# Three of the four late gate blocks issued ahead of the sparse attention, each in a PSUM bank of its own

## The chip, the cores and the metric

One core of one Trainium2 chip runs the kernel. The metric is the device time of one execution in microseconds (us). The core's engines are named here as the profile names them: PE (TensorE, matmuls), PEld (its weight loads), DVE (VectorE), ACT (ScalarE), POOL (GpSimd) and SP (SyncE, whose queue issues nearly all transfers; SPq in the rows). Sums of matmuls are formed in PSUM, eight banks of 128x512 float32.

## The reference

A decoder block on 1024 tokens of width 1024, float32. Cut to what matters here:

```python
hn = rms_norm(h, attn_norm_g[l])
proj = hn @ w_in[l]
aq, ak, av, bq, bkv, iq, ik, iw, gates = jnp.split(proj, IN_SPLITS, axis=-1)
gates = jax.nn.sigmoid((gates + b_gates[l]).astype(jnp.float32)).astype(h.dtype)
gate_a, gate_b = jnp.split(gates, 2, axis=-1)
o_a = sliding_window_sink_attention(aq, ak, av, sinks[l], bias_a)
...
o_b = indexed_sparse_mla(q_abs, c_kv, iq, ik, iw, w_uv[l], bias_b)
mixed = gate_a * (o_a @ w_branch_a[l]) + gate_b * (o_b @ w_branch_b[l])
h = h + mixed @ w_out[l]
h = h + (jax.nn.silu(hn @ w_ffn_gate[l]) * (hn @ w_ffn_up[l])) @ w_ffn_down[l]
```

The gates are 2048 columns of the projection: 16 blocks of 128 columns, each for two halves of 512 tokens. Nothing but `mixed` reads them.

## The kernel before

Float32 products are made of three matmuls on split operands (high, low): high by high, high by low, low by high. A gate block for one half of the tokens is 8 slices of the width by 3, so 24 matmuls of 128x512 into one PSUM bank (`gate`, L905; `mm3`, L202, L193). Then ACT takes the tanh out of the bank (L914), POOL scales it (L915) and SP stores it in DRAM (L916, `gate_dram`). Its weights come in two chunks (`weights`, L168): SP loads a raw chunk of 256 KB (L185, `w_raw`, two buffers), ACT makes the high part (L187, `w_hi`), POOL the low part (L188, `w_lo`); the split parts have four buffers, so two blocks' weights are there at a time.

The program runs in phases. `phase1` has the projections, the choice of keys and the window attention; in it `gates` (L894) makes 28 of the 32 gate blocks as filler between other matmuls. Blocks 12 to 15 of the second half (`LATE = 4`) are left for `phase_b` (L919), the sparse attention. That phase has four pairs of heads, four units of 256 queries in each (`sparse_block`, L983). For each pair `keys_values` (L951) loads keys and values: the two heads' keys one after the other through one raw buffer `kraw` (ACT casts `kb`, L689, DVE takes the low part, L690), the values through `vraw` (L960 to L962), the meta tokens' values through `mraw` (L967 to L970). `queries` (L973) loads `qraw` and splits it on ACT (L979) and DVE (L980). A unit then has scores on PE (L1007, banks `s`), the masked row minimum on DVE (L1011, `pb`), the exponential on ACT (L1014), transposes on PE (L1038, banks `tp`) with the split on ACT and DVE (L127, L133), and the weighted values on PE (L1049 to L1052, bank `pv`). In this phase the banks are three `s`, three `tp`, one `pv` and one `gps` (the gates and branch A).

The order is found by a scheduler at build time from the order in which the program is written, the readiness of operands and buffers, and marks: a matmul issued with a mark may not be placed before the instruction that the mark names. Each engine then runs its own list in that order. `branch_a` (L1074), written behind the 16 units, makes the four late blocks and then branch A's product; its matmuls are filler for the units. Of the 96 gate matmuls the first 30 (`LFREE`) have no mark, the other 66 have marks spread over the first fifth (`LEND`) of the marked matmuls of the phase:

```python
n = LATE * KC * 3
marks = iter([self.marks[int(len(self.marks) * LEND * (i - LFREE) / (n - LFREE))] if i >= LFREE else None for i in range(n)])
for c in range(16 - LATE, 16):
    self.gate(c, 1, self.gate_weights(c), marks)
```

Branch A's own matmuls have marks from 0.1 to 0.85 of the phase, behind the loads of the window attention's output (`wa_raw`, L1065), which go into the buffers of the normed input that the last gate block frees.

Of the kernel before, what the change touches and what calls it, by code (L numbers as in the profile page):

```python
# [21 lines left out]
KC = D // P  # L22
# [34 lines left out]
GSP = (64, 180, 250)  # L57
GEND = 0.97
LATE = 4
LFREE = 30  # L60
LEND = 0.2
B2 = (0.85, 1.1)

# [40 lines left out]
class Program:  # L104
# [797 lines left out]
            for half in range(2 if c < 16 - LATE else 1):  # L902
                self.gate(c, half, w, marks, 2 * c + half >= MMG)

    def gate(self, c, half, w, marks, both=False):  # L905

        nc = self.nc
        b0 = self.col["b_gates"]
        self.turn = not self.turn
        pool, tag = (self.mm, "ps") if both and self.turn else (self.gp, "gps")  # L910
        ps = pool.tile([P, 512], F32, name=tag, tag=tag)
        self.feature_cols(ps, w, slice(0, P), NM + 512 * half, 512, marks)
        t = self.wg.tile([P, 512], F32, name="gt", tag="gt", bufs=2)
        nc.scalar.activation(t, ps, AF.Tanh, scale=0.5, bias=self.vec[:, b0 + c:b0 + c + 1])  # L914
        nc.gpsimd.tensor_scalar(t, t, 0.5, 0.5, op0=ALU.mult, op1=ALU.add)  # L915
        nc.sync.dma_start(self.gate_dram[half][c], t)  # L916


    def phase_b(self):  # L919
        nc, I = self.nc, self.I  # L920
        self.psum(0, *BP, 1, 1)
        self.marks = []
        with self.pool("kv", side="right") as kvp, self.pool("slb", side="right") as wp:
            qlo = [wp.tile([P, 2, 256], F32R, name=f"qlo{k}") for k in range(2)]
            for t in qlo:
                self.clear_lo(t)
            first = self.queries(wp, 0, ORDER[0][0], qlo[0])
            pm = [wp.tile([P, 256], F32R, name=f"pm{k}") for k in range(4)]
            self.vm = [wp.tile([P, 2, P], F32R, name=f"vm{k}") for k in range(2)]
            for t in self.vm:  # L930
                self.clear(t.rearrange("p h d -> p (h d)"))
            for t in pm:
                self.clear(t)
            self.unit, self.mixed, self.wb = 0, [], {}
            kv = self.keys_values(kvp, 0)
            for pr in range(4):
                kb, vb = kv
                bt = wp.tile([P, 2, 256], F32, name="bt_b", tag="bt_b", bufs=2)
                self.load_bias(bt, 1, 2 * pr)
                for i, sb in enumerate(ORDER[pr]):  # L940
                    q = self.queries(wp, pr, sb, qlo[i % 2]) if pr + i else first
                    self.sparse_block(wp, pr, sb, q, kb, vb, pm, bt)
                    if i == 0 and pr < 3:
                        kv = self.keys_values(kvp, pr + 1)
            self.branch_a()
            n = KC * 4 * 3
            at = [B2[0] + (B2[1] - B2[0]) * i / n for i in range(n)]
            self.branch_b(0, self.wg, iter([self.marks[min(len(self.marks) - 1, int(len(self.marks) * a))] for a in at]))
        self.mask_es.close()
# [124 lines left out]
    def branch_a(self):  # L1074

        nc, I = self.nc, self.I
        n = LATE * KC * 3
        marks = iter([self.marks[int(len(self.marks) * LEND * (i - LFREE) / (n - LFREE))] if i >= LFREE else None for i in range(n)])
        for c in range(16 - LATE, 16):
            self.gate(c, 1, self.gate_weights(c), marks)  # L1080
        pool = self.wg
        o = [self.load_o(pool, [self.oa_dram[half][:, c] for c in range(4)], 2, lo_pool=False, ring=self.xhp) for half in range(2)]
        n = KC * 2 * 4 * 3
        b0 = BSP[0]
        marks = iter([self.marks[int(len(self.marks) * (b0 + (BSP[1] - b0) * i / n))] for i in range(n)])
        for m in range(KC):
            w = self.weights(pool, I["w_branch_a"][0][:, P * m:P * m + P].rearrange("(k p) n -> p k n", p=P), raw_pool=pool, unit=512, bufs=WB)
            for half in range(2):
                hc = slice(512 * half, 512 * half + 512)
                ps = self.gp.tile([P, 512], F32, name="gps", tag="gps")  # L1090
                self.mm3(ps, [(*w[k], *o[half][k]) for k in range(4)],
                         marks)
                t = pool.tile([P, 512], F32, name="gt", tag="gt", bufs=2)
                g = pool.tile([P, 512], F32, name="ga", tag="ga", bufs=2)
                nc.sync.dma_start(g, self.gate_dram[half][m])
                nc.scalar.copy(t, ps)
                nc.gpsimd.tensor_mul(t, t, g)
                nc.sync.dma_start(self.ya_dram[half][m], t)
# [450 lines left out]
```

## Time and profile before

| | |
|---|---|
| median of 3 runs | 1499.91 us (1499.42 to 1502.9) |
| the profiled execution | 1500.29 us, span 1498.5 us |
| PE busy | 1388.4 us, 93% of the span |
| DVE / ACT / POOL busy | 990.8 / 818.1 / 648.8 us (66 / 55 / 43%) |
| granted TensorE clock, mean | 0.969 of full |
| first and last scores of the sparse attention (L1007) | 498.1 and 683.5 us |

The span is what the trace covers, from its first instruction to its last. The profiled execution took 1.8 us more than its span and lies 0.4 us above the median of the runs.

### The profile page before, as it was taken

Reading aid. Unit: us, or ns where it says so; the run is one execution under the profiler, and the core shown is the slowest. Engines: PE = TensorE matmul, PEld = TensorE weight load, DVE = VectorE, ACT = ScalarE, POOL = GpSimd, SP = SyncE. Lnnn points to the kernel's source line nnn. Section 1 sums busy time; section 2 is a strip of 40 time slices with the busy share of each in tenths; the row PEclk is TensorE's granted clock in tenths of the full one; section 3 lists DMA queues with packets and bytes.
Section 4 is the critical chain, followed back from the end, with each engine's and each line's share of the span. In section 5 each row is a group of like instructions: output and inputs, shape, how many; then the busy total and the mean of one; then the engine's idle time right before and its main releaser. Section 6 shows DMA issues by size and latency. Waiting matters only on the chain.

```text
span 1498.5 us, 21232 instructions
## 1 busy us (share of the span) xinstructions
PE 1388.4 (93%) x6847; PEld 1157.7 (77%) x6847; DVE 990.8 (66%) x2122; ACT 818.1 (55%) x1743; POOL 648.8 (43%) x823
## 2 busy tenths in 40 slices
PE   4999787999799799999899699999999999999997
PEld 3988785777587688888687478888888888888886
DVE  6258998036576787777697995444544447696585
ACT  5347684994688677886335643333333333444473
POOL 4137465666666557675300015555555555000004
PEclk9999888999899899999999899999999999999999
DMA  6421121246443845335931133332333338832332
GB/s 202 142 68 39 29 65 43 87 135 209 112 140 105 212 133 173 119 117 179 308 138 57 56 112 102 103 109 95 105 106 106 106 102 292 323 99 98 117 109 113
DMA packets 148038, 189.79 MB, mean 127 GB/s; under 512 B 11331, under 2 KB 95126, under 8 KB 147670
## 3 DMA queue, kind: packets, MB, share of 16 engines
q1 hardware_dynamic: 147568, 188.28, 39.1%
q8 instruction: 54, 0.88, 0.3%
q14 instruction: 58, 0.48, 0.1%
q10 hardware_dynamic: 198, 0.14, 0.0%
q0 software_dynamic: 160, 0.01, 0.0%
HBM read 133.49 MB, written 58.03 MB: 128 GB/s over the span
## 4 chain that ended last, share of the span: by engine, by line
PE 64%; DVE 14%; issue 6%; ACT 6%; DMA 5%; POOL 5%; SPq 1%; POOLq 0%; ACTq 0%; DVEq 0%
PE ps L193 25%; PE s L193 23%; PE gps L193 7%; DVE mask L815 4%; ACT mask L857 2%; PE pv L1049 2%; PE s L1007 2%; PE tp L1038 2%; DMA ga<-gate_dram 1%; PE tp L198 1%; POOL y L1510 1%; PE pv L193 1%; DMA kraw<-bk_dram 1%; DMA wa_raw<-in_w_in 1%; DVE hb L1267 1%
## 5 line engine op out<-in xcount | busy, mean ns | idle before, releaser
L1360 POOL TENSOR_TENSOR fhl<-fr,fhl 128x512 fp32r<-128x512 f32 x60 | 97.5, 1645 | 223.0 <-ACT fhl L1359 223.0
L1360 POOL TENSOR_TENSOR fhl<-fs,fhl 128x512 fp32r<-128x512 f32 x80 | 106.5, 1355 | 106.8 <-ACT fhl L1359 106.8
L188 POOL TENSOR_TENSOR w_lo<-w_raw,w_hi 128x512 fp32r<-128x512 f32 x60 | 81.2, 1356 | 93.9 <-ACT w_hi L187 75.8
L193 PE MATMUL s<-ht,fhl 128*128 128x512 f32 x384 | 121.8, 393 | 0.0
L193 PE MATMUL ps<-ht,fhl 128*128 128x512 f32 x320 | 101.1, 392 | 0.0
L193 PE MATMUL gps<-oh,w_hi 128*128 128x512 f32 x232 | 94.2, 406 | 4.1 <-ACT gt L914 4.1
L857 ACT ACTIVATE mask<-high,smallg 128x784 bf16<-128x784 uint16 (+3 forms) x66 | 70.2, 1063 | 46.1 <-POOL smallg L866 28.4
L193 PE MATMUL gps<-ol,w_hi 128*128 128x512 f32 x232 | 92.7, 399 | 0.0
L193 PE MATMUL gps<-oh,w_lo 128*128 128x512 f32 x232 | 92.1, 397 | 0.0
L193 PE MATMUL s<-yhl,fhl 128*128 128x512 f32 x396 | 90.6, 389 | 0.0
L193 PE MATMUL ps<-yhl,fhl 128*128 128x512 f32 x396 | 90.2, 389 | 0.0
L1430 ACT CAST yhl<-wd 128x512 fp32r<-128x512 f32 x66 | 41.1, 622 | 89.9 <-PE ps L193 50.2
L193 PE MATMUL s<-h,fhl 128*128 128x512 f32 x272 | 87.7, 393 | 0.8 <-DVE hb L1267 0.5
L193 PE MATMUL ps<-h,fhl 128*128 128x512 f32 x256 | 82.9, 395 | 5.1 <-ACT h L1317 5.1
L133 DVE TENSOR_TENSOR ptl<-tp,pth 128x512 fp32r<-128x512 f32 (+2 forms) x112 | 70.9, 645 | 23.9 <-ACT pth L127 22.6
L193 PEld LDWEIGHTS s<-yhl,fhl 128*128 128x128 f32 x396 | 74.3, 188 | 15.5
L193 PEld LDWEIGHTS ps<-yhl,fhl 128*128 128x128 f32 x396 | 74.3, 188 | 15.4
L193 PEld LDWEIGHTS s<-ht,fhl 128*128 128x128 f32 x384 | 72.0, 188 | 17.2 <-ACT fhl L1359 0.7
L865 POOL TENSOR_SCALAR smallg<-smallg 128x1 f32<-128x1 f32 x128 | 58.9, 463 | 59.9 <-ACT mask L857 59.5
L1359 ACT CAST fhl<-fr 128x512 fp32r<-128x512 f32 x66 | 39.8, 619 | 76.6 <-issue 36.1
L1431 DVE TENSOR_TENSOR yhl<-wd,yhl 128x512 fp32r<-128x512 f32 x66 | 45.6, 691 | 50.2 <-ACT yhl L1430 50.2
L193 PE MATMUL s<-lt,fhl 128*128 128x512 f32 x192 | 75.3, 392 | 0.0
(479 smaller groups left out, 4267.5 us busy)
## 6 DMA issues: line engine op xcount, KB each, us to landing
fr<-in_w_ffn_gate SPq DMA_DIRECT2D x22, 512.0 KB, 4.0
fr<-in_w_ffn_up SPq DMA_DIRECT2D x22, 512.0 KB, 4.5
wd<-in_w_ffn_down SPq DMA_DIRECT2D x44, 256.0 KB, 5.1
da<-acts SPq DMA_DIRECT2D x44, 256.0 KB, 3.6
w_raw<-in_w_in SPq DMA_DIRECT2D x40, 256.0 KB, 3.0
act<-a SPq DMA_DIRECT2D x33, 256.0 KB, 2.1
da<-act SPq DMA_DIRECT2D x33, 256.0 KB, 4.3
acts<-s SPq DMA_DIRECT2D x33, 256.0 KB, 2.0
```

The lines of the kernel that those rows point to most:

```text
L133: nc.vector.tensor_sub(lo, ps, hi.bitcast(F32))
L188: (nc.vector if lo_dve else nc.gpsimd).tensor_sub(t[1], t[2], t[0].bitcast(F32))
L193: mm = self.nc.tensor.matmul(*args, **kw)
L815: nc.vector.tensor_scalar(self.mask[j], src[j], at[:, i:i + 1], None, op0=op, op1=ALU.add, accum_out=out[:, i:i + 1])
L857: nc.scalar.activation(self.mask[j], src[j], AF.Sign, bias=at[:, i:i + 1], scale=scale, accum_out=out[:, i:i + 1])
L865: g.tensor_scalar(c[:, o], acc[:, o], bar[:, o], b[:, o], op0=ALU.is_ge, op1=ALU.subtract)
L1007: nc.tensor.matmul(ps[:, :n], q[k][:, h, qc:qc + P], kb[:, h, at:at + n], start=k == 0, stop=k == 1)
L1038: mm = nc.tensor.transpose(pt[:, P * i:P * i + P], prs[par, e][:, NM + P * rr:NM + P * rr + P], self.ident)
L1359: nc.scalar.copy(hi, a[name])
L1360: (nc.gpsimd if q else nc.vector).tensor_sub(lo, a[name], hi.bitcast(F32))
L1430: nc.scalar.copy(hi, src)
L1431: nc.vector.tensor_sub(lo, src, hi.bitcast(F32))
```

## The change

The constant `LFREE` goes. Before the sparse attention's first `keys_values`, blocks 12, 13 and 14 are written with no mark, in the banks `gps`, `tp` and `s`. Block 15 stays in `branch_a`, its 24 matmuls with marks over the same first fifth.

```diff
-LFREE = 30
...
-    def gate(self, c, half, w, marks, both=False):
+    def gate(self, c, half, w, marks, both=False, bank=None):
...
-        pool, tag = (self.mm, "ps") if both and self.turn else (self.gp, "gps")
+        pool, tag = bank or ((self.mm, "ps") if both and self.turn else (self.gp, "gps"))
...
             self.unit, self.mixed, self.wb = 0, [], {}
+            for c, ring in zip(range(16 - LATE, 16), ((self.gp, "gps"), (self.tp, "tp"), (self.sp, "s"))):
+                self.gate(c, 1, self.gate_weights(c), iter([None] * 3 * KC), bank=ring)
             kv = self.keys_values(kvp, 0)
...
-        n = LATE * KC * 3
-        marks = iter([self.marks[int(len(self.marks) * LEND * (i - LFREE) / (n - LFREE))] if i >= LFREE else None for i in range(n)])
-        for c in range(16 - LATE, 16):
+        n = (LATE - 3) * KC * 3
+        marks = iter([self.marks[int(len(self.marks) * LEND * i / n)] for i in range(n)])
+        for c in range(19 - LATE, 16):
             self.gate(c, 1, self.gate_weights(c), marks)
```

The number of instructions on each engine stays the same. The lists of the engines are alike up to the last block of the window attention and differ from there through the first four units. Counted from the first late gate matmul, the filler matmuls (gates and branch A) in PE's list stand like this at the end of units 1 to 5: before 35, 48, 72, 108, 144, with the change 74, 82, 91, 108, 144; behind the fourth unit the counts stay within 2 of each other. Line numbers of the change lie 1 lower up to L931 and 1 higher from there to L1075.

First place, PE at the end of the window attention. `pv_4078` is its last product; `gps_7662` before is block 12, and in the change `gps_5160` is block 12 and `tp_5201` block 13. Before:

```order
L193 MATMUL gps_5071<-xt0_198,w_lo_5066 128x512
L193 MATMUL pv_4078<-pth_4084,va_3070 128x512
L193 MATMUL pv_4078<-ptl_4085,va_3070 128x512
L193 MATMUL pv_4078<-pth_4095,va_3070 128x512
L193 MATMUL pv_4078<-ptl_4096,va_3070 128x512
L193 MATMUL gps_7662<-oh_182,w_hi_7650 128x512
L193 MATMUL gps_7662<-ol_183,w_hi_7650 128x512
```

and with the change:

```order
L192 MATMUL tp_5201<-oh_188,w_lo_5190 128x512
L192 MATMUL pv_4078<-pth_4084,va_3070 128x512
L192 MATMUL pv_4078<-ptl_4085,va_3070 128x512
L192 MATMUL pv_4078<-pth_4095,va_3070 128x512
L192 MATMUL pv_4078<-ptl_4096,va_3070 128x512
L192 MATMUL tp_5201<-oh_190,w_hi_5195 128x512
L192 MATMUL tp_5201<-ol_191,w_hi_5195 128x512
L192 MATMUL gps_5160<-oh_182,w_hi_5148 128x512
```

Twelve matmuls of block 13 now stand ahead of the window attention's last product and two behind it; block 12 follows them with its 24, then the other 10 of block 13 and the 24 of block 14, and only then the first scores.

Second place, ACT from the tanh of the last block of `phase1` (`gt_5096`) to the first queries (`qhi_5133`). `w_hi_7732` before and `w_hi_5230` in the change are the first chunk of block 14's weights; its buffer is the one that block 12's first chunk leaves. Before:

```order
L914 ACTIVATE gt_5096<-gps_5071,vec_281 128x512
L759 COPY o_4101<-pv_4078 64x256 x2
L689 CAST kb_5148<-kraw_5150 128x1040
L187 CAST w_hi_7732<-w_raw_7734 128x512
L961 CAST vb_5149<-vraw_5160 128x16x64
L187 CAST w_hi_7738<-w_raw_7740 128x512
L914 ACTIVATE gt_7687<-gps_7662,vec_281 128x512
L969 CAST vm0_5140<-mraw_5164 16x64 x2
L979 CAST qhi_5133<-qraw_5130 128x512
L689 CAST kb_5148<-kraw_5155 128x1040
```

and with the change, with `w_hi_7773` and `w_hi_7779` for block 15:

```order
L186 CAST w_hi_5230<-w_raw_5232 128x512
L688 CAST kb_5271<-kraw_5273 128x1040
L758 COPY o_4101<-pv_4078 64x256
L962 CAST vb_5272<-vraw_5283 128x16x64
L758 COPY o_4101<-pv_4078 64x256
L186 CAST w_hi_5236<-w_raw_5238 128x512
L688 CAST kb_5271<-kraw_5278 128x1040
L186 CAST w_hi_7773<-w_raw_7775 128x512
L913 ACTIVATE gt_5185<-gps_5160,vec_281 128x512
L962 CAST vb_5390<-vraw_5401 128x16x64
L186 CAST w_hi_7779<-w_raw_7781 128x512
L913 ACTIVATE gt_5226<-tp_5201,vec_281 128x512
```

The cast for block 14 moved ahead of the first keys' cast, and five more casts and tanhs of the gates, with the next pair's values (`vb_5390`), stand ahead of the first queries, which follow two rows further on. On DVE the first row minimum before stands behind the second head's keys (`kb_5148`); in the change the zero fills stand behind those keys, and the next pair's keys (`kb_5389`) ahead of the first row minimum.

Third place, SP's queue from the first head's keys (`kraw_5150` before, `kraw_5273` in the change) to the first queries and the next pair's keys (`kraw_5391` in the change). Before:

```order
L916 DMA gate_dram015_124<-gt_5096 128x512
L967 DMA mraw_5164<-bv_dram_82 16x64
L751 DMA oa_dram1_84<-o_4101 128x2x128
L185 DMA w_raw_7740<-in_w_in 128x4x128
L660 DMA kraw_5155<-bk_dram0_78 64x1040
L660 DMA qraw_5130<-bq_dram00_68 64x2x256 x2
L660 DMA kraw_5155<-bk_dram0_78 64x1040
L300 DMA bt_b_5171<-bias_dram1_487 128x2x256
```

and with the change:

```order
L184 DMA w_raw_7775<-in_w_in 128x4x128
L659 DMA kraw_5278<-bk_dram0_78 64x1040 x2
L961 DMA vraw_5401<-bv_dram_82 128x8x128
L750 DMA oa_dram1_84<-o_4101 128x2x128
L184 DMA w_raw_7781<-in_w_in 128x4x128
L659 DMA qraw_5130<-bq_dram00_68 64x2x256 x2
L299 DMA bt_b_5294<-bias_dram1_487 128x2x256
L659 DMA kraw_5391<-bk_dram1_79 64x1040
L915 DMA gate_dram112_137<-gt_5185 128x512
L659 DMA kraw_5391<-bk_dram1_79 64x1040
```

Both chunks of block 15 (`w_raw_7775`, `w_raw_7781`) and the next pair's values now stand ahead of the first queries, and the store of block 12 stands between the two halves of the next pair's keys.

## Rows read from the trace of the kernel before

**Rows 1.** The page: the span, and each engine's busy us, share and instructions.
```profile
span 1498.5 us, 21232 instructions
...
PE 1388.4 (93%) x6847; PEld 1157.7 (77%) x6847; DVE 990.8 (66%) x2122; ACT 818.1 (55%) x1743; POOL 648.8 (43%) x823
```

**Rows 2.** Windows: stretch, length, busy us of each engine (instructions), PEclk, DMA share, GB/s.
```profile
498.50:509.80 11.30, 7.55 (x30) 5.75 (x29) 10.02 (x28) 8.62 (x22) 9.18 (x16) 0.68 0.96 235
...
518.70:562.00 43.30, 40.86 (x253) 36.40 (x254) 36.57 (x110) 33.24 (x65) 22.34 (x37) 0.96 0.46 131
...
540.00:552.00 12.00, 12.00 (x77) 10.74 (x76) 11.54 (x30) 10.46 (x19) 6.03 (x9) 1.00 0.64 183
```

**Rows 3.** Timeline of PE: start us, us, instruction, [idle before <-releaser].
```profile
485.41 0.47 PE L193 MATMUL pv<-pth,va 128*128 128x512 f32 x1 [0.24 <-DVE o L760]
...
486.42 0.49 PE L193 MATMUL gps<-oh,w_hi 128*128 128x512 f32 x1
...
491.75 0.39 PE L193 MATMUL gps<-oh,w_lo 128*128 128x512 f32 x1
495.81 0.79 PE L193 MATMUL gps<-oh,w_hi 128*128 128x512 f32 x1 [3.68 <-ACT gt L914]
...
498.54 0.59 PE L1007 MATMUL s<-kb,qhi 128*128 128x144 f32 x2
```

**Rows 4.** Timeline of ACT at the start of the sparse attention.
```profile
489.33 1.07 ACT L689 CAST kb<-kraw 128x1040 fp32r<-128x1040 f32 x1 [1.49 <-DMA kraw<-bk_dram]
...
492.22 1.04 ACT L961 CAST vb<-vraw 128x1024 fp32r<-128x1024 f32 x1 [1.31 <-DMA vraw<-bv_dram]
494.43 0.62 ACT L187 CAST w_hi<-w_raw 128x512 fp32r<-128x512 f32 x1 [1.16 <-DMA w_raw<-in_w_in]
495.07 0.69 ACT L914 ACTIVATE gt<-gps,vec 128x512 f32<-128x512 f32 x1
...
497.18 0.62 ACT L979 CAST qhi<-qraw 128x512 fp32r<-128x512 f32 x1
...
502.07 0.41 ACT L1014 ACTIVATE pb<-pb,st 128x144 f32<-128x144 f32 x1
...
515.39 1.06 ACT L689 CAST kb<-kraw 128x1040 fp32r<-128x1040 f32 x1 [1.70 <-DMA kraw<-bk_dram]
```

**Rows 5.** Timeline of DVE, the same stretch.
```profile
490.43 1.24 DVE L690 TENSOR_TENSOR kb<-kraw,kb 64x1040 fp32r<-64x1040 f32 x1 [2.14 <-ACT kb L689]
...
494.56 0.76 DVE L155 CAST qlo<-zero 64x512 fp32r<-64x512 f32 x2
...
498.20 0.68 DVE L980 TENSOR_TENSOR qlo<-qraw,qhi 64x512 fp32r<-64x512 f32 x1
...
500.95 0.31 DVE L1011 CUSTOM_DVE_ANT_0 pb<-s,near 128x144 f32<-128x144 f32 x1
...
516.49 1.24 DVE L690 TENSOR_TENSOR kb<-kraw,kb 64x1040 fp32r<-64x1040 f32 x1 [1.28 <-ACT kb L689]
...
518.69 0.47 DVE L1011 CUSTOM_DVE_ANT_0 pb<-s,mask,st 128x256 f32<-128x256 f32 x1
```

**Rows 6.** Timeline of POOL: a gate's low weights, and the scaling of a gate.
```profile
495.12 1.33 POOL L188 TENSOR_TENSOR w_lo<-w_raw,w_hi 128x512 fp32r<-128x512 f32 x1 [2.04 <-ACT w_hi L187]
496.42 0.66 POOL L915 TENSOR_SCALAR gt<-gt 128x512 f32<-128x512 f32 x1
```

**Rows 7.** Timeline of SP's queue: when the key and query loads were issued.
```profile
491.70 0.45 SPq L660 DMA_DIRECT2D kraw<-bk_dram  x1
492.20 1.26 SPq L660 DMA_DIRECT2D qraw<-bq_dram  x2
493.50 0.60 SPq L660 DMA_DIRECT2D kraw<-bk_dram  x1
```

**Rows 8.** DMA issues from 470 to 530 us: KB each, median us to landing.
```profile
kraw<-bk_dram SPq DMA_DIRECT2D x10, 260.0 KB, 3.6
qraw<-bq_dram SPq DMA_DIRECT2D x14, 128.0 KB, 3.9
...
vraw<-bv_dram SPq DMA_DIRECT2D x3, 512.0 KB, 5.9
```

## The prediction

> **What bounds the kernel now.** I read the page first: PE is busy 93% of the span [rows 1], so a change that leaves PE's work as it is can only move PE's idle time and its clock. The windows say where that idle time lies. From 518.7 to 562 us, four units long, PE is busy 40.86 of 43.30 us [rows 2]; there the filler matmuls cost their full time. At the start of the sparse attention it is otherwise: from 498.5 to 509.8 us PE is busy 7.55 of 11.30 us at a granted clock of 0.68, so for part of the time at its lower level of 1.2 GHz, with the transfers busy at 0.96 and DVE for 10.02 us [rows 2]. In PE's timeline the reader sees the idle time just before it: gate block 12 runs from 486.42 to 491.75, then PE stands for 3.68 us until the tanh has emptied the one bank [rows 3]. ACT's timeline tells why: the tanh stood at 495.07 behind a weight cast at 494.43, which had waited 1.16 us for its load [rows 4], though the bank had been full since about 492.
>
> In block 12 twenty-three steps take 491.75 - 486.42 = 5.33 us [rows 3], so a gate matmul at full clock is **0.232 us**. PE was free for late gates at 485.41 - 0.24 = 485.17.
>
> **The change, part by part.** All instructions stay; what changes is where the 72 matmuls of three blocks, their casts, tanhs, scalings, stores and weight loads stand. There are two terms: a later start of the sparse attention, and less filler in its third and fourth unit.
>
> *Term A, the start.* PE itself would be through with its three blocks at 485.17 + 76 x 0.232 = 502.8 (72 of them and four products of the window attention). But ACT's list now holds block 14's first cast ahead of the first keys' cast. Its buffer is free only when block 12's first 12 matmuls are done, and PE has 12 of block 13, 4 products and 2 more of block 13 ahead of these: 485.17 + 30 x 0.232 = 492.1, where before that buffer was left at 486.42 + 12 x 0.232 = 489.2 and nothing waited. ACT's keys then end at 492.1 + 0.62 + 1.07 = 493.8 (0.62 and 1.07 from [rows 4]); before, at 490.4. From there one raw key buffer sets the pace:
>
> - DVE's low part, 1.24 [rows 5]: 495.1. SP issues the second head's keys twice, 0.45 each [rows 7]: 496.0. They land 3.6 later [rows 8]: 499.6. ACT casts them, 1.06 [rows 4]: 500.7.
> - Behind that cast, ACT has block 15's first chunk, 0.62, and block 12's tanh, 0.69 [rows 4]: 502.0. POOL makes the low weights, 1.33, then the scaled gate, 0.66 [rows 6], with the memsets between: about 503.6.
> - SP's list has the gate's store between the two halves of the next pair's keys. Store and second half take about 0.9: 504.5. Landing, 3.6: 508.1. ACT's cast 1.06 and DVE's low part 1.24: **510.4**. This low part stands ahead of the first row minimum on DVE, which before began at 500.95 [rows 5].
>
> So the first row minimum comes 510.4 - 500.95 = **9.5 us later**, by the list alone. Beside this chain, and hidden by it, run the first queries: block 14's second cast and block 15's load are through by about 498, the loads of the queries take 1.26 and 3.9 [rows 7, 8], landing near 503.5; the next pair's values, issued before them, land near 502.8 (5.9 [rows 8]) and ACT has values 1.04, cast 0.62, tanh 0.69 and queries 0.62 [rows 4] ahead, so the queries are split near 507. DVE's zero fills, 3.6 us from 494.56 to 498.20 [rows 5], moved behind the second keys, and end near 505. If the key chain were shorter, these would set the start at about 508. The banks cost nothing: block 14's tanh empties its scores bank right behind the last key cast, before 510.4.
>
> The keys that are early now are not waited for later: the idle 1.70 us of ACT and 1.28 us of DVE at 515.39 and 516.49 [rows 4, 5], on the way to the third unit's row minimum at 518.69, go. What is late next there is DVE's own work of two units, so I take 1.5 back: **+8** at 518.7, with 9.5 and 6.5 (both idle pieces gone) as ends.
>
> *Term B, the filler.* By the two lists, 40 late filler matmuls stood ahead of that row minimum, and 77 now; at the end of the fourth unit both have 108. So 37 x 0.232 = 8.6 us of filler leave the stretch 518.7 to 562. They free their full time only until another engine bounds the stretch. DVE has 36.57 us of work in its 43.30 [rows 2], so at most 6.7 can go; at the least nothing, if PE's idle time only grows. In the twelve microseconds of this phase where DVE is best filled it reaches 11.54 of 12.00, 96% [rows 2]. I take 94%, near that end because DVE's order is not disturbed here: 36.57 / 0.94 = 38.9, a gain of **4.4**.
>
> Behind the fourth unit the lists agree within two matmuls, so the shift stays. Sum: 8 - 4.4 = +3.6, on the profiled 1500.29 that is **1503.9 us**. The profiled execution lies 0.4 us above the median of the runs.
>
> One rule bears on term A. The row shows that a ready tanh stood behind a cast that waited for its load [rows 4]. The Trainium skill (PSUM — Partial Sum Buffer, section Engine vs sequencer instructions) says that the queues of ScalarE, VectorE and GpSimdE are strictly first in, first out; the trace agrees, by that 1.16 us. Could ACT pass a waiting instruction, the sum would be that of the first rival.
>
> **The rivals.**
>
> *Faster.* The waits that I add up along the lists may be shorter: the landing of 3.6 us was measured while the transfers were busy at 0.96 [rows 2], and the loads now stand further apart. If the start is set by PE alone, it is 502.8 - 500.95, about +2, and term B at its bound gives -6.7: -4.7, **1495.6 us**. For it: PE has no 3.68 us of idle time any more, and works without a stop to 502.8. Then the clock may hold too: 7.55 busy us at 0.68 would be 7.55 x 0.68 = 5.1 at full, 2.4 us less, for 1493.2. Against it: the single raw key buffer. It decides whether the first exponential, at 502.07 before [rows 4], comes before about 504. The Trainium skill (TensorE: Matmul & The Clock Gate, section HAM oscillation — how this bites in real kernels) has idle stretches drop the array to half rate; the window at 0.68 agrees, and by that rule the unbroken gates speak for this rival up to 502.8, my own gap behind them against it.
>
> *Slower.* The start is late by 9.5 and nothing comes back: PE has no filler in the gap between its gates' end at 502.8 and the first scores, and little in units 1 to 4, the clock falls as it did at 0.68 [rows 2], and the chain from keys over DVE and ACT to the transposes sets units 3 and 4 in place of PE. Then 1500.3 + 9.5 = **1509.8 us**. It decides if PE's busy share in those units falls while they take their 43 us as before. For it: PE's 0.96 clock there already shows some loss. Against it: DVE's 84% in that stretch leaves room.
>
> *Nothing.* The late start is just what the missing filler gives back, since the filler had only filled PE's waiting time anyway: **1500.3 us**. It is so where PE's total idle time up to the end of unit 4 stays alike; then the first row minimum is late by 4 to 7 us and unit 4 ends at 562.
>
> **How the numbers follow.** About 0.3%, 4.5 us, is what a measurement of this kernel can tell from no change; same thus reaches from 1495.4 to 1504.4. My forecast has a chance of 0.45; its own range, 1500.1 (+6.5 - 6.7) to 1507.6 (+9.5 less half of 4.4), lies 0.27 within and 0.18 above. The faster rival has 0.22, of which 0.18 is beyond the bound; the slower 0.18, 0.17 beyond; the hidden one 0.15, with 0.02 faster. Faster 0.20, same 0.45, slower 0.35. The range goes from 1494.4, the middle of the first rival's two values, to 1509.8, the second's.
>
> **What would show each step.** Right, if ACT in the changed trace idles before block 14's cast until near 492 and names PE; if the second head's keys are cast near 500; if PE has a gap from about 503 and the first row minimum comes near 510; if units 3 and 4 then take about 39 us with DVE above 90% and no idle time of ACT and DVE for keys. Term A is wrong if the first exponential comes before 506, term B if PE is still above 94% busy in units 3 and 4. The whole is wrong if the stretch behind the fourth unit, whose lists agree, changes by more than a microsecond or two.

## The result, and the profile after

The changed kernel is slower: 1509.26 us median of 6 runs (1506.78 to 1510.69) against 1501.4 us of 6 runs of the kernel before, ratio 1.0055 (95% interval 1.0042 to 1.0069). Two more sets of the same pair, below, gave 1.0022 (1.0003 to 1.0040) and 1.0030 (1.0017 to 1.0043). By all three it costs some 3 to 8 us (the lowest interval begins at 0.5); 3.6 were forecast.

The page of the changed kernel, span and engines, answers to [rows 1]:

```profile
span 1507.4 us, 21231 instructions
PE 1394.8 (93%) x6847; PEld 1161.8 (77%) x6847; DVE 997.3 (66%) x2122; ACT 818.3 (54%) x1743; POOL 648.2 (43%) x823
```

The shares tell nothing. The traces do, once both have the same zero. I count from the tanh of the last block of `phase1` on ACT, at 485.66 us before and here at:

```profile
488.20 0.69 ACT L913 ACTIVATE gt<-gps,vec 128x512 f32<-128x512 f32 x1
```

What lies ahead of that instruction is alike in both programs; its place is scatter, as the repeats show. A unit's end is taken where its last product with the meta tokens' values begins. From the tanh, in us, with the repeats' traces as second and third value:

| | before | change | later by (means) |
|---|---|---|---|
| first row minimum (DVE) | 15.3, 14.8 | 23.4, 22.7, 23.3 | 8.1 |
| row minimum that opens the third unit's rows | 33.0, 32.7 | 39.3, 39.0, 39.5 | 6.4 |
| unit 4 ends (PE) | 80.8, 80.6 | 86.5, 86.2, 88.4 | 6.3 |
| unit 5 ends | 102.8, 103.5 | 105.1, 104.8, 107.0 | 2.5 |
| unit 8 ends | 133.3, 135.0 | 135.4, 135.0, 137.2 | 1.7 |
| unit 16 ends | 219.9, 221.6 | 223.9, 223.6, 225.8 | 3.7 |
| first store of the next stage (`h_dram`, SP) | 319.0, 321.2 | 322.0, 324.6, 325.2 | 3.8 |

At the ends of these units equally many filler matmuls are done in both (108 at the fourth, 144 at the fifth, 324 at the sixteenth), so the last column compares like with like there.

**The start.** ACT's timeline of the changed kernel answers to [rows 4]:

```profile
490.31 0.62 ACT L186 CAST w_hi<-w_raw 128x512 fp32r<-128x512 f32 x1 [1.42 <-POOL gt L914]
...
492.39 1.06 ACT L688 CAST kb<-kraw 128x1040 fp32r<-128x1040 f32 x1 [1.47 <-DMA kraw<-bk_dram]
...
499.67 1.06 ACT L688 CAST kb<-kraw 128x1040 fp32r<-128x1040 f32 x1 [2.88 <-DMA kraw<-bk_dram]
...
506.34 0.62 ACT L980 CAST qhi<-qraw 128x512 fp32r<-128x512 f32 x1
508.13 1.06 ACT L688 CAST kb<-kraw 128x1040 fp32r<-128x1040 f32 x1 [1.18 <-DMA kraw<-bk_dram]
...
511.95 0.41 ACT L1015 ACTIVATE pb<-pb,st 128x144 f32<-128x144 f32 x1 [0.68 <-DVE st L1012]
```

The cast for block 14 did not hold the first keys: it ran at 490.31, right behind PE's twelfth matmul of block 13 (490.06), and the keys' cast then waited 1.47 us for its own load. The row names POOL as releaser, whose scaling ended at 490.13. Block 12's first matmul began only at 491.67, so the buffer that this cast filled can't be the one that block 12's first chunk leaves, as the change was described; by the times it is block 13's. DVE's timeline, which answers to [rows 5], shows what set the start:

```profile
493.49 1.24 DVE L689 TENSOR_TENSOR kb<-kraw,kb 64x1040 fp32r<-64x1040 f32 x1 [5.68 <-ACT kb L688]
...
500.77 1.24 DVE L689 TENSOR_TENSOR kb<-kraw,kb 64x1040 fp32r<-64x1040 f32 x1 [3.31 <-ACT kb L688]
501.93 2.56 DVE L154 CAST qlo<-zero 64x512 fp32r<-64x512 f32 x2
504.50 1.89 DVE L150 CAST vm<-zero 128x256 fp32r<-128x256 f32 x2
506.31 1.13 DVE L150 CAST pm<-zero 128x256 fp32r<-128x256 f32 x4
507.36 1.47 DVE L963 TENSOR_TENSOR vb<-vraw,vb 128x1024 fp32r<-128x1024 f32 x1
508.75 1.15 DVE L981 TENSOR_TENSOR qlo<-qraw,qhi 64x512 fp32r<-64x512 f32 x1
509.94 1.63 DVE L689 TENSOR_TENSOR kb<-kraw,kb 64x1040 fp32r<-64x1040 f32 x1
511.60 0.31 DVE L1012 CUSTOM_DVE_ANT_0 pb<-s,near 128x144 f32<-128x144 f32 x1
```

DVE stands 5.68 and 3.31 us for keys, and from 500.77 works without a gap to the first row minimum: second keys, zero fills, the next pair's values, queries, the next pair's keys. PE's timeline gives the other side; its last gate matmul begins at 504.62, without a stop before it, and then:

```profile
504.62 0.39 PE L192 MATMUL s<-oh,w_lo 128*128 128x512 f32 x1
507.01 0.50 PE L1008 MATMUL s<-kb,qhi 128*128 128x144 f32 x2 [2.00 <-ACT qhi L980]
509.96 0.81 PE L1008 MATMUL s<-kb,qlo 128*128 128x144 f32 x2 [2.45 <-DVE qlo L981]
...
555.72 0.63 PE L1039 MATMUL tp<-ident,pb 128*128 128x128 f32 x4 [1.95 <-DVE ptl L132]
```

**Units 3 and 4.** From the row minimum that opens the third unit's rows to the end of unit 4 the kernel before takes 47.8 us, the change 47.2, though it has 37 filler matmuls less there. The windows of both, first this stretch and then unit 5 (columns as in [rows 2]); before:

```profile
518.70:566.50 47.80, 45.36 (x277) 40.27 (x277) 40.62 (x121) 37.74 (x74) 25.44 (x42) 0.96 0.48 140
566.50:588.50 22.00, 20.38 (x136) 18.24 (x135) 16.03 (x49) 16.76 (x40) 14.84 (x27) 1.00 0.41 126
```

and with the change:

```profile
527.50:574.70 47.20, 41.84 (x254) 35.75 (x253) 44.46 (x133) 38.49 (x80) 23.37 (x48) 0.93 0.39 117
574.70:593.30 18.60, 18.60 (x126) 16.91 (x125) 12.49 (x36) 15.09 (x34) 13.52 (x22) 1.00 0.53 164
```

PE has 23 matmuls less in this stretch by the trace and not 37, because some of unit 5's scores and transposes already stand there, and with the clock at 0.93 in place of 0.96 its busy time fell by 3.5 us only. DVE's rose by 3.8, to 94% of the stretch: 1.9 of it are low parts of branch A's input, most of the rest row minima that unit 5 then has less. That DVE took the bound over is argued from this share. It isn't all: the third trace needs 48.9 us for the same DVE work, with longer waits for keys, and a second key buffer (`kraw2_after`, below) brings the stretch to 44.8. What was done ahead came back in unit 5: DVE has 3.5 us less to do there, PE 1.8, and PE is busy without a break, 18.6 us in place of 22.0.

**Units 9 to 16.** Here the change loses some 2 us more, and the traces say by what. PE's list from the end of unit 8 to that of unit 16 is, by the names of the tiles, the same in the kernel before and in `early1`, below; another one is the same in the change, `one_bank`, `kraw2_before` and `fills_kraw2`. The first takes 86.6 to 86.8 us in its three traces, the second 88.5 to 88.6 in its six, whatever stands ahead. In this order: before, `early1`, the change, `kraw2_before`:

```profile
619.00:705.60 86.60, 85.38 (x576) 76.97 (x575) 65.64 (x204) 66.83 (x156) 56.61 (x99) 1.00 0.44 137
624.60:711.40 86.80, 85.53 (x577) 77.08 (x576) 65.79 (x204) 66.83 (x156) 56.76 (x99) 1.00 0.44 137
623.60:712.10 88.50, 85.54 (x572) 76.48 (x571) 66.68 (x199) 66.32 (x154) 55.50 (x95) 1.00 0.42 131
617.90:706.40 88.50, 85.55 (x572) 76.51 (x571) 66.58 (x198) 66.14 (x153) 55.65 (x95) 1.00 0.43 132
```

PE's busy time is alike and its clock full; the second order has 1.7 us more of PE's waiting. Which of its places cost that wasn't tried.

### The profile page after: what moved, and what is told of

It is laid out like the page before. It is cut to its first block, busy times and chain, and to the rows that moved or that the text cites. A ratio compares the mean times of both kernels' runs of the same rounds, so it can differ in the third digit from the quotient of the medians.

```text
span 1507.4 us, 21231 instructions
## 1 busy us (share of the span) xinstructions
PE 1394.8 (93%) x6847; PEld 1161.8 (77%) x6847; DVE 997.3 (66%) x2122; ACT 818.3 (54%) x1743; POOL 648.2 (43%) x823
## 4 chain that ended last, share of the span: by engine, by line
PE 60%; DVE 14%; issue 7%; DMA 6%; ACT 6%; POOL 5%; SPq 1%; POOLq 0%; DVEq 0%; ACTq 0%
PE ps L192 24%; PE s L192 20%; PE gps L192 7%; DVE mask L814 3%; ACT mask L856 2%; PE pv L1050 2%; PE tp L1039 2%; PE s L1008 2%; DMA ga<-gate_dram 1%; POOL smallg L864 1%; DMA x<-in_x 1%; POOL y L1511 1%; PE tp L197 1%; PE pv L192 1%; DVE hb L1268 1%
## 5 line engine op out<-in xcount | busy, mean ns | idle before, releaser
L1431 ACT CAST yhl<-wd 128x512 fp32r<-128x512 f32 x66 | 41.1, 622 | 90.2 <-PE ps L192 48.9
L192 PE MATMUL gps<-oh,w_hi 128*128 128x512 f32 x216 | 87.2, 404 | 1.0 <-ACT gt L913 1.0
L192 PE MATMUL gps<-ol,w_hi 128*128 128x512 f32 x216 | 86.4, 400 | 0.0
L192 PE MATMUL gps<-oh,w_lo 128*128 128x512 f32 x216 | 85.7, 397 | 0.0
```

The lines of the kernel that those rows point to most:

```text
L192: mm = self.nc.tensor.matmul(*args, **kw)
L1431: nc.scalar.copy(hi, src)
```

## The experiments

Ratios are to the kernel before, run beside each on the same chip.

**The same two kernels again.** `before_again`, no edit:

> The kernel before once more, for a second trace of it. The two traces at hand differ by 2.5 us ahead of the first late gate and by 3.3 us behind the store of the normed stream, where the programs are alike. If that is scatter from execution to execution, this trace lies somewhere else than the first: the tanh of the last block of phase1 not at 485.7 or the time from the first norm store to the end not 693.9 us, by 1 us or more. If it belongs to the change, both agree with the first trace within 0.5 us.

The tanh is at 484.3 and the time from the first norm store (the last row of the table) to the end 695.5 us: 1.4 and 1.6 us from the first trace. Scatter.

`after_again`, no edit:

> The changed kernel once more, for a second trace and more times. Scatter: the tanh of the last block of phase1 lies elsewhere than 488.2, and the time behind the first norm store differs from 697.2 us. Belonging to the change: both within 0.5 us. In either case the first row minimum comes 23.4 us behind that tanh (511.6 - 488.2; before 15.3), and the median is 1507 to 1511.

Median 1506.74 us of 12 runs, ratio 1.0022 (1.0003 to 1.0040), just under the 1507 to 1511 expected. The tanh at 488.1 repeats the first trace, the time behind the store (695.0) does not; the first row minimum comes 22.7 us behind the tanh, 23.4 expected.

`after_third`, no edit:

> The changed kernel a third time, beside the next three on one chip. The first two sets of times put it 7.5 and 3.6 us (means) above the kernel before. If the two traces of each tell the whole effect (end of the sparse attention's last unit 2 us later, counted from the tanh that ends phase1, with 3 filler matmuls, 0.7 us, still to do), it is 2 to 5 us above the kernel before. If also the parts in which the programs are alike are longer for it (rival), it is 6 to 9 above.

Median 1506.8 us of 12 runs, ratio 1.0030 (1.0017 to 1.0043), so 4.5 us: the first reading. The tanh now lies at 483.2, so what the alike parts showed in the first trace was scatter, and the table above holds the effect.

**How much the start and the banks matter.** `one_bank`:

```diff
-((self.gp, "gps"), (self.tp, "tp"), (self.sp, "s"))
+((self.gp, "gps"),) * 3
```

> The three blocks written first and without marks as in the change, but all three in the bank gps. In ACT's list the first keys' cast then stands ahead of block 14's cast again, and 48 filler matmuls instead of 72 stand ahead of the first scores. If the late start of the rows is what costs (theory), the first row minimum comes 4 us or more nearer to the tanh of phase1's last block than with three banks, and the time is 1502 to 1506. If the loss is that filler is missing in units 1 to 4 whatever the start (rival), the units get about the same filler as with the change from unit 2 on, and the time stays within 1.5 us of the change's 1509.

Median 1507.92 us, ratio 1.0023 (1.0008 to 1.0038); the change beside it had 1506.74. The first row minimum comes 17.5 us behind the tanh, 5.6 earlier than the mean with three banks, and still unit 4 ends at 85.8 and unit 16 at 223.3, 1.2 and 1.1 below the change's means. The rival: an early first row by itself wins little.

`early1` and `early2`, one or two blocks written first, the others left in `branch_a` (the edit for one):

```diff
-for c, ring in zip(range(16 - LATE, 16), ((self.gp, "gps"), (self.tp, "tp"), (self.sp, "s"))):
+for c, ring in zip(range(16 - LATE, 16), ((self.gp, "gps"), (self.tp, "tp"), (self.sp, "s"))[:1]):
...
-n = (LATE - 3) * KC * 3
+n = (LATE - 1) * KC * 3
...
-for c in range(19 - LATE, 16):
+for c in range(17 - LATE, 16):
```

> Only block 12 is written first and without marks; blocks 13 to 15 stay in branch_a, their 72 matmuls with marks over the first fifth of the phase. Against the kernel before only the 6 matmuls of block 13 that stood unmarked ahead of the first scores move, so PE need not wait there for the one bank. Theory (what is lost comes from blocks 13 and 14 ahead of the scores): -2 to +1 us against the kernel before, and no wait of 3.68 us in PE's timeline. Rival (taking marked filler out of its place is what costs, by whatever amount): slower than before by 2 us or more.

Median 1506.9 us, ratio 1.0029 (1.0015 to 1.0043): as slow as the change, though only six matmuls left the place ahead of the scores (with the other engines' lists moved as well), and its first row minimum (14.5) is as early as before. The rival's figure holds. The wait of 3.68 us is gone from PE, but two others stand in its place; the third unit's rows open 36.4 us behind the tanh, 3.5 later than before:

```profile
498.03 0.81 PE L1008 MATMUL s<-kb,qhi 128*128 128x144 f32 x2 [5.64 <-ACT qhi L980]
...
504.72 1.14 PE L1008 MATMUL s<-kb,qhi 128*128 128x400 f32 x3 [3.07 <-ACT qhi L980]
```

> Blocks 12 and 13 first, 14 and 15 in branch_a with their 48 matmuls over the same fifth of the marks. With one block early the time was 4.7 us above the kernel before (means), with three 4.6. Theory (the number of early blocks only moves PE's waiting, and what remains comes from small waits further on): also 2 to 6 us above. Rival (one early block is too few to fill the start, three too many): within 2 us of the kernel before.

Median 1509.95 us of 5 runs, ratio 1.0038 (1.0025 to 1.0050), 5.4 us. One, two and three blocks early cost alike within their intervals; no number of early blocks stands out.

`banks_only`, the kernel before with another bank for block 13:

```diff
-    self.gate(c, 1, self.gate_weights(c), marks)
+    self.gate(c, 1, self.gate_weights(c), marks, bank=(self.tp, "tp") if c == 17 - LATE else None)
```

> The kernel before with block 13 in a bank of tp, nothing else: its 6 unmarked matmuls need not wait for block 12's tanh, by which PE stood 3.68 us. Theory (PE's waiting at the start is set by keys and queries, not by the bank): PE's wait of 3.68 us goes to the first scores, and the time is within 1.5 us of the kernel before. Rival (the bank was the limit there): 2 to 4 us faster.

Median 1559.47 us, ratio 1.0369 (1.0353 to 1.0384): neither. From the end of unit 3 to that of unit 15 its filler stands still at 48 matmuls, and the rest runs behind the units. Why the order came out so wasn't tried. But the trace gives an estimate of a price, though the order differs too: with 67 filler matmuls the sixteen units end 185.2 us behind the tanh, with 324 in the kernel before at 219.9. That is 34.7 us for 257 matmuls, 0.135 each in place of the 0.232 that one takes [rows 3].

`no_gates`, the change without its three blocks:

```diff
-    self.gate(c, 1, self.gate_weights(c), iter([None] * 3 * KC), bank=ring)
+    t = self.wg.tile([P, 512], F32, name="gt", tag="gt", bufs=2)
+    nc.gpsimd.memset(t, 0.5)
+    nc.sync.dma_start(self.gate_dram[1][c], t)
```

> Blocks 12 to 14 of the second half are left out: no weights, matmuls, tanh or scaling, only a store of a constant in their place. 72 matmuls of 0.232 us are 16.7 us of PE. If these blocks cost their full time wherever they stand, the kernel is 16.7 us faster than with the change and some 12 faster than before. Theory (the kernel before hid part of them in PE's waiting, the change hides none ahead of the scores but gives units 1 to 4 nothing to fill their waits with): 8 to 13 us below the kernel before, and PE waits in units 1 to 4 as in the changed kernel, with the stretch from the first row minimum to the end of unit 4 within 3 us of the change's 63 to 65.

Median 1497.76 us, ratio 0.9953 (0.9939 to 0.9966): only 6.8 us below the kernel before, less than either reading had. Three blocks with 16.7 us of matmuls cost the kernel before 6.8 (interval 5.1 to 9.2); some 10 then lie in waits that PE has anyway. The price is that of whole blocks, since their loads, casts and tanhs are left out as well, and of an order that shifts with them; in the one trace, counted from the tanh, unit 16 ends only some 4 us earlier than before. PE's timeline without the three blocks shows the waits at the start:

```profile
498.36 0.81 PE L1010 MATMUL s<-kb,qhi 128*128 128x144 f32 x2 [11.03 <-ACT qhi L982]
502.55 0.49 PE L1010 MATMUL s<-kb,qhi 128*128 128x144 f32 x1 [2.67 <-DVE kb L689]
...
506.39 0.93 PE L1010 MATMUL s<-kb,qhi 128*128 128x400 f32 x2 [2.35 <-ACT qhi L982]
```

The first wait of 11.03 us has room for 47 matmuls of 0.232; the kernel before puts 30 there, the change 72. Its first row minimum (16.5) is no earlier than with 30. From there to the end of unit 4 it takes 58.7 us, 4.4 to 6.4 less than in the change's three traces (63.1, 63.5, 65.1), so "within 3 us" was missed too.

**Repairs.** `fills_next`, the zero fills and the next pair's keys and values put back by marks, on DVE and, for the next pair's casts, on ACT:

```diff
+            with self.tc.issue_after(after) if after else nullcontext():
-        nc.vector.tensor_sub(dst[64:], raw[64:], dst[64:].bitcast(F32))
+                nc.vector.tensor_sub(dst[64:], raw[64:], dst[64:].bitcast(F32))
...
-            kv = self.keys_values(kvp, 0)
+            kv = self.keys_values(kvp, 0, after=self.filled)
...
-                        kv = self.keys_values(kvp, pr + 1)
+                        kv = self.keys_values(kvp, pr + 1, *([self.first_min] * 2 if pr == 0 else []))
```

> The change, with two things put back where DVE had them before: the zero fills ahead of the second head's keys (low part), and the next pair's keys and values behind the first row minimum. PE's gates, their three banks and their place stay. Theory (DVE's list sets the start: in the changed trace DVE works without a gap from 500.8 to the first row minimum at 511.6): the first row minimum comes 4 to 5 us earlier, and most of it reaches the end: 1504 to 1506. Rival (keys and queries arrive too late anyway, or what is won at the start is lost again in units 1 to 4): the first row minimum moves by under 1.5 us, or it moves and the end of unit 4 does not, and the time stays at 1508 to 1511.

Median 1504.95 us, ratio 1.0004 (0.9989 to 1.0019); 1.8 us below the change beside it, with intervals that overlap. The first row minimum, below, comes 20.3 us behind the tanh (485.37), 2.8 earlier: between theory and rival. Unit 4 ends at 85.6, unit 8 at 136.4, unit 16 at 222.7. DVE's list was part of the late start, but at unit 8 nothing of that is left (mean of the change 135.9). What this kernel is ahead at unit 16 comes from units 9 to 16, where its list is its own and takes 86.3 us.

```profile
505.64 0.29 DVE L1015 CUSTOM_DVE_ANT_0 pb<-s,near 128x144 f32<-128x144 f32 x1
```

`kraw2_after` and `kraw2_before`, a second raw key buffer in the sparse attention:

```diff
-        raw = pool.tile([P, (NB + 1) * P], F32, name="kraw", tag="kraw", bufs=1)[:, :C]
+        raw = pool.tile([P, (NB + 1) * P], F32, name="kraw", tag="kraw", bufs=bufs)[:, :C]
...
-            self.stacked(kvp, kb[:, e], self.bk_dram[pr][64 * e:64 * e + 64])
+            self.stacked(kvp, kb[:, e], self.bk_dram[pr][64 * e:64 * e + 64], 2)
```

> The change with two raw key buffers in the sparse attention instead of one. In the changed trace PE stands 1.95 us at 553.6, while ACT's list holds a transposed block's cast behind a key cast that waits 2.16 us for its load; that load was issued only when the one raw buffer was free. Theory (the stall of units 4 and 5 and the late start hang on the one raw buffer): these waits go, the first row minimum comes 2 to 4 us nearer to the tanh of phase1's last block, and the time falls by 3 to 6 us against the change. Rival (PE's waiting moves on to the next wait, since DVE's work in these units sets the pace): the time falls by less than 1.5 us.

Median 1503.92 us, ratio 1.0009 (0.9994 to 1.0023); 2.9 below the change beside it. What it repairs is the wait of units 4 and 5. In the changed kernel ACT's list holds the transposed block behind a key cast that waits for its load:

```profile
552.52 1.06 ACT L688 CAST kb<-kraw 128x1040 fp32r<-128x1040 f32 x1 [2.16 <-DMA kraw<-bk_dram]
553.49 0.58 ACT L126 CAST pth<-tp 128x512 fp32r<-128x512 f32 x1
```

and PE stands 1.95 us until 555.72, when DVE, behind that cast, has emptied a bank (2.05 and 2.99 in the repeats). With two buffers the wait there is:

```profile
556.99 0.52 PE L1039 MATMUL tp<-ident,pb 128*128 128x128 f32 x3 [0.76 <-DVE ptl L132]
```

Unit 4 ends at 84.5 and unit 5 at 102.7, 2.5 and 2.9 earlier than the change's means. The start moved only from 23.1 to 22.1, against 2 to 4 expected. So a gain came in unit 4, not at the start. But unit 8 ends at 136.0, no earlier than the change's mean of 135.9: the gain doesn't last. What this kernel is ahead at the end (unit 16 at 222.3, mean of the change 224.4) comes from units 9 to 16, 86.3 us in an order of its own. The time was close to what the theory said, by another way.

> The kernel before with two raw key buffers. The same waits are in its trace (0.85, 1.70 and 1.01 us at 505.7, 515.4 and 547.6, 1.99 at 599.4), but PE has filler there. Theory that filler hides them: within 1.5 us of the kernel before. Rival (they cost as much as in the changed kernel): 2 to 4 us faster.

Median 1504.05 us, ratio 1.0014 (1.0002 to 1.0026): 1.8 us slower, so neither, though the interval reaches down to 0.3 us. At unit 8 it isn't late (132.9, before 133.3 and 135.0); it loses in units 9 to 16, where its PE list is that of the change and takes the same 88.5 us.

`fills_kraw2`, both edits together:

> The change with both repairs: zero fills and next pair's keys as DVE had them, and two raw key buffers. Alone they took 2.6 and 2.7 us off the change (means). Theory (two separate waits, each with its price): together about 5 us off the change, so within 1.5 us of the kernel before, and the end of unit 4 (last product with the meta tokens' values) at most 83 us behind the tanh of phase1's last block, against 86 to 88 with the change and 81 before. Rival (one and the same waiting, seen in two places): not more than 3 us off the change, 2 us or more above the kernel before.

Median 1515.56 us, ratio 1.0076 (1.0062 to 1.0090): slower than the change, which neither reading foresaw; the rival's bounds hold, its reason doesn't. In ACT's list the next pair's key cast now stands ahead of the second queries and waits 3.44 us for a load that SP issued at 507.14 and 508.30:

```profile
512.83 1.06 ACT L689 CAST kb<-kraw 128x1040 fp32r<-128x1040 f32 x1 [3.44 <-DMA kraw<-bk_dram]
...
514.32 1.14 ACT L983 CAST qhi<-qraw 128x512 fp32r<-128x512 f32 x2
```

PE waits for these queries:

```profile
514.99 0.70 PE L1011 MATMUL s<-kb,qhi 128*128 128x400 f32 x1 [4.85 <-ACT qhi L983]
```

None of the repairs is faster than the kernel before.

## Why the prediction was right, and where it was not

Sign and size held: +3.6 us was forecast, 8.3, 3.3 and 4.5 were measured (the ratios on 1502 us), and the median of every set lies in the range, the first by 0.5 us. The steps did less well than the sum, and that the sum came out so near is luck: errors of opposite sign.

- **PE's own time**: 502.8 forecast for the end of the gates. The last one began at 504.62, with a tanh 2.5 us later in this execution than before: right.
- **Term A, the way**: the step "Its buffer is free only when block 12's first 12 matmuls are done" failed. By the times the cast ran when block 13's first 12 were done, 2.1 us behind the tanh, and held no key. Moved to the clock of before (2.54 us less), the first keys' cast ended at 490.9 and not 493.8, the second head's at 498.2 and not 500.7, the next pair's at 506.7 and not 509.2.
- **Term A, the size**: 9.5 was forecast for the first row minimum, 8.1 measured. DVE's own list filled the place that the key chain left. I had the fills ending near 505 on the clock of before, and they did (504.9), by luck: they began 2.5 us earlier than I had them and took 5.5 us where I took 3.6, because the first one took 2.56 us in place of 0.76. And I ran them beside the chain, whereas values, queries and keys queue behind them. At the third unit's rows 8 was forecast, 6.4 measured, below my lower end of 6.5.
- **Key waits**: "The keys that are early now are not waited for later" failed. ACT waits 1.18, 1.26 and 2.16 us for keys at 508.13, 518.42 and 552.52; the last of these stops PE, and is thus a part of what term B lacks.
- **Term B** is the step of the sum that failed where it stood: 4.4 us were to come back in units 3 and 4, and 0.1 came. DVE did reach the 94% that I took, but I had kept its work as it was, and it rose from 40.62 to 44.46 us in the like stretch; nor did PE lose all 37 matmuls. The slower rival foresaw the outcome: units 3 and 4 take their time as before, with PE no longer the bound. My stretch was also read wrongly: 518.7 to 562 isn't four units, and unit 4 ends at 566.5. With 47.80 us and 40.62 of DVE the same sum gives 4.6 in place of 4.4, so this isn't what failed.
- **"Behind the fourth unit the lists agree within two matmuls, so the shift stays"** failed as well, both ways: 3.8 us came back in unit 5, because DVE and PE had done part of its rows before unit 4 was over, and some 2 us were lost again in units 9 to 16, where the counts agree within two but PE's order does not (86.6 us and 88.5). Equal counts of filler on PE mean neither that the order is the same nor that the other engines stand alike. By the last sign that the prediction gave, a change behind the fourth unit of more than a microsecond or two, its account as a whole was wrong.

So the sum was 6.3 - 3.8 + 1.2 = 3.7 at the end of the sixteenth unit, and not 8 - 4.4. The faster rival's condition, a first exponential before about 504, fell: 511.95, or 509.4 on the clock of before. The rival of no change had the mechanism that `no_gates` then showed, filler that lies in PE's waits, and was off by those 3.7 us.

What stays open is which places of the order cost the time. Orders that end alike, 4 to 5 us above the kernel before, lose it at different places: `early1` is 3.5 us late at the third unit's rows and has the order of before in units 9 to 16, the change has lost 1.7 us at unit 8 and loses 2.0 there. The runs show that neither the first row's time nor the number of early blocks decides it; they show no common cause.

## What to carry to other kernels

Filler costs its full time only where the filled engine would not have waited: here three blocks with 16.7 us of matmuls cost 6.8, and a version without them tells this in one run. Before filler is moved, set the length of the wait (11 us) against what goes into it (16.7 us), and write down what the other engines' lists put beside it, since a list that moves takes casts, fills and loads along. Two repairs that alone ended 2 to 3 us below the change ended together 11 us above the kernel before, so repairs of an order have to be measured together. And compare the lists themselves behind the place that you moved, not only counts: one order of units 9 to 16 took 1.9 us more than the other in every trace, whatever stood ahead of it.

## What was not expected of the hardware

The first zero fill, two casts of 64x512, took 0.76 us before [rows 5] and 2.56 in the change (2.55 and 2.56 in its repeats). It started at 501.93 while POOL was in a subtraction that took 1.84 us where the same one took 1.33 [rows 6]:

```profile
501.33 1.84 POOL L187 TENSOR_TENSOR w_lo<-w_raw,w_hi 128x512 fp32r<-128x512 f32 x1 [3.17 <-ACT w_hi L186]
```

The Trainium skill (SBUF — State Buffer, section Who interferes with whom) says that VectorE and GpSimd share a pair of ports: a cast of VectorE can need the pair, and then the one that comes second waits for the whole of the other's instruction; a VectorE instruction with two inputs in SBUF contends with a GpSimd one that reads SBUF. The two rows agree with that: DVE's second keys run to 502.01 and lengthen POOL's subtraction, and this one ends at 503.17 and holds the fill. Two other traces agree as well. In `no_gates` no such subtraction runs beside the fill, in `early1` one runs from 493.96 to 495.44; the fill in the first, then in the second:

```profile
494.80 0.76 DVE L154 CAST qlo<-zero 64x512 fp32r<-64x512 f32 x2
494.35 2.13 DVE L154 CAST qlo<-zero 64x512 fp32r<-64x512 f32 x2
```

No run changes only this, so the cause is argued, not shown.

PE's clock fell behind a short wait. After the 1.95 us ahead of 555.72 and the two smaller ones behind it, PE is busy for the whole of the next ten microseconds, at a granted clock of 0.84, so for part of it at 1.2 GHz and not at 2.4:

```profile
550.00:560.00 10.00, 6.94 (x39) 5.53 (x38) 9.59 (x26) 7.06 (x14) 2.93 (x7) 0.82 0.60 164
560.00:570.00 10.00, 10.00 (x64) 9.34 (x63) 8.71 (x23) 8.39 (x18) 5.87 (x9) 0.84 0.18 58
```

A stretch of the kernel before, with PE busy 7.99 of 10 us, kept 1.00; what divides the two isn't shown:

```profile
555.00:565.00 10.00, 7.99 (x47) 6.59 (x46) 8.70 (x27) 8.47 (x16) 6.02 (x9) 1.00 0.56 167
```
